# FF1's input operands made one product ahead, and GpSimd without sums, low parts and affine steps up to the early chunks

## The chip, the core and the metric

The kernel runs on one core of a Trainium2 chip. The metric is device time in microseconds for one execution. TensorE (PE) multiplies; VectorE (DVE), ScalarE (ACT) and GpSimd (POOL) do the elementwise work; SyncE (SP) issues the transfers.

## What is computed

One layer of a streaming encoder, 1024 frames by 1024 channels, float32, with conditioning from a vector c. After a first part (projection, retention and gated linear attention, giving `mixed`), what matters here is:

```python
m = mixed @ w_out
x = _layer_norm(ALPHA * x + gate1 * m, ln1_w, ln1_b)
u2 = _layer_norm(x) * (1.0 + scale2) + shift2
f = square(relu(u2 @ w_ff1)) @ w_ff2          # w_ff1 1024 x 4096, w_ff2 4096 x 1024
x = _layer_norm(ALPHA * x + gate2 * f, ln2_w, ln2_b)
```

## The kernel before

**Three products for one.** A float32 product is made as three matmuls of a shorter type. `split` (lines 203 to 206) makes of each operand a high part (a cast on ScalarE, L205) and a low part (source less high part, L206, on VectorE or GpSimd), and `mm3` adds high by high (L211), low by high (L212) and high by low (L213). Inputs have the parts `uhp` and `ulp`, FF1's weights `w1h` and `w1l`.

**Out-projection and norms.** A loop over 8 tiles of 128 frames makes two halves of each by matmuls (`out_part`; VectorE adds x to the half in PSUM and gives y, L838), then takes the first norm of the tile before (`first_norm`, with statistics by bn_stats L200 and L201, a reciprocal root in small steps L181 to L190) and the parameter-free norm (`normed`) of the tile before that. `affine` (L848 to L860) applies the norm's weight and bias to a half, xn: half 0 by ScalarE and two GpSimd steps (L855, L856), half 1 by two VectorE steps (L858, L859). The second norm's statistics (bs<-xn, L200) need both halves.

**The transposed input.** `u2_half(h)` transposes four normed tiles on TensorE (L878) and evicts 8 blocks `ub`, even ones on VectorE (L884), odd ones on ScalarE (L882). Half 0 comes after the out-projection's last tile, half 1 ahead of chunk 2's first products.

**FF1.** w_ff1 is worked through in NC = 8 chunks by a scheme of seven products in place of eight, in the order (1, 2, 5, 6, 7, 3, 4). Products 1 and 2 take blocks of input and weights as they are; the others take sums or differences of blocks, of the input (`RIGHT`) and of the weights (`LEFT`), some of them made in place of an earlier one (`term`, L914). `input_operand(i)` makes the four input operands of product i for all chunks: four sums where it has one (ut, or ub in place), then each one's high and low part. `ff1` makes the two weight operands of a product (w1t or raw in place, then w1h and w1l), and issues its 24 matmuls. After a product VectorE or ScalarE takes the result out of PSUM (`kept`, L1005 and the additions L1019, L1036, L1041), and `hidden` applies relu and square.

**The early chunks.** EARLY = 3: products 1 and 2 of chunks 0, 1 and 2 come first (`ff1_first`), as they need half 0 of the input; then all input operands of products 5, 6, 7, 3 and 4 are made; then follow, chunk by chunk, the five other products (`ff1_rest`, a generator that yields after each product).

**Who does a sum or a low part.** `pick(share)` keeps a running sum of shares and gives a piece to GpSimd whenever the sum reaches 1, otherwise to VectorE. S_U and L_U are the shares for the sums and low parts of the inputs, S_A and L_A for those of the weights of chunks 0 to 2, S_R and L_R for FF2. All pieces count on one running sum.

**Order on an engine.** The program's order gives each piece its place; a scheduler then settles the order of instructions on each engine, and each engine works in order.

Of the kernel before, what the change touches and what calls it, by code (L numbers as in the profile page):

```python
# [13 lines left out]
AF = mybir.ActivationFunctionType  # L14
ALU = mybir.AluOpType
# [13 lines left out]
NRAW = 15  # L29
NLATE = 6  # L30

S_U, L_U = 0.3, 0.3
S_A, L_A = 0.3, 0.3
S_B, L_B = 0.0, 0.2
S_R, L_R = 0.4, 0.4

# [43 lines left out]
def layer_kernel(ctx: ExitStack, tc, x, c, w_ada, b_ada, w_in, ret_norm_w, gla_gate_w, gla_gate_b,  # L80
                 gla_norm_w, w_out, ln1_w, ln1_b, w_ff1, w_ff2, ln2_w, ln2_b, cosT, sinT, cst, out, gam):
    nc = tc.nc
    V, A, G, T = nc.vector, nc.scalar, nc.gpsimd, nc.tensor
# [11 lines left out]
    def nm(s):  # L95
        uid[0] += 1
        return f"{s}_{uid[0]}"
# [10 lines left out]
    def S(shape=(P, HALF), dt=F32, n="s"):  # L108
        tag, bufs = TAGS.get(n, ("S", None))
        return sp.tile(list(shape), dt, tag=tag, name=nm(n), bufs=bufs)  # L110
# [13 lines left out]
    def small(n, tag, bufs=4):  # L124
        return sm.tile([P, n], F32, tag=tag, name=nm(tag))
# [147 lines left out]
    def ada_row(cols, dst):  # L273
        acc = ada_sum(ada_load(cols, ada_late), range(NK))
        yield
        ps = mxt()
        T.matmul(ps, lhsT=ones, rhs=acc, start=True, stop=True)
        br = ada_late()
        nc.sync.dma_start(out=br, in_=b_ada[0:1, cols:cols + HALF].partition_broadcast(P))
        V.tensor_tensor(out=dst, in0=ps, in1=br, op=ALU.add)  # L280
        yield
# [3 lines left out]
    def ada(step):  # L285

        for p in pending:
            next(p)
        pending[:] = [step] if step else []
        for p in pending:  # L290
            next(p)
# [75 lines left out]
    for kind in ("gqk0", "gqk1", "rqk0", "rqk1", "rqk2", "rqk3"):  # L367
        i = int(kind[3])
# [39 lines left out]
    for _ in range(SHARES[0][0]):  # L408
        i = next(steps)
# [334 lines left out]
    row = {}  # L744

    def rowt(name):
        row[name] = [S(n=name), S(n=name)]
        return row[name]
# [92 lines left out]
    def norm_stats(parts):  # L841
        mv, rs = small(2, "mv"), small(1, "rs1")
        stats(parts, mv)
        for _ in row_rsqrt(rs, mv[:, 1:2]):
            pass
        return mv[:, 0:1], rs

    def affine(src, mean, rs, w, b, q):  # L848

        r = S(n="xn")  # L850
        if q == 0:
            nb = small(1, "nb1")
            V.tensor_scalar(out=nb, in0=mean, scalar1=-1.0, scalar2=rs, op0=ALU.mult, op1=ALU.mult)
            A.activation(r, src, AF.Identity, bias=nb, scale=rs)
            G.tensor_tensor(out=r, in0=r, in1=w, op=ALU.mult)  # L855
            G.tensor_tensor(out=r, in0=r, in1=b, op=ALU.add)  # L856
        else:
            V.scalar_tensor_tensor(out=r, in0=src, scalar=mean, in1=w, op0=ALU.subtract, op1=ALU.mult)  # L858
            V.scalar_tensor_tensor(out=r, in0=r, scalar=rs, in1=b, op0=ALU.mult, op1=ALU.add)  # L859
        return r  # L860

    def first_norm(t, ys):

        mean, rs = norm_stats(ys)
        xn = [affine(ys[q], mean, rs, row["ln1_w"][q], row["ln1_b"][q], q) for q in range(2)]
        for q in range(2):
            x1d[t][q] = dr.tile([P, HALF], F32, tag=f"x1d{t}_{q}", name=nm("x1d"))
            nc.sync.dma_start(out=x1d[t][q], in_=xn[q])
        return xn
# [22 lines left out]
    ORDER = (1, 2, 5, 6, 7, 3, 4)  # L892
# [14 lines left out]
    def term(rules, i, blocks, new, share):  # L907

        rule = rules[i]
        if len(rule) == 2:  # L910
            return blocks[rule]
        op, a, b, place = rule
        res = new() if place is None else blocks[place]
        pick(share).tensor_tensor(out=res, in0=blocks[a], in1=blocks[b], op=op)  # L914
        blocks[i] = res
        return res

    def operand(src, new, share):
        hi, lo = new("h"), new("l")
        split(src, hi, lo, lo_eng=pick(share))  # L920
        return hi, lo
# [13 lines left out]
    def load_ff1(c, hh):  # L935
        for kh in range(2):
            for n in range(2):
                w = raw(W1S)
                last_load[0] = nc.sync.dma_start(out=w, in_=w1v[2 * kh + n, :, :, 2048 * hh + 256 * c:2048 * hh + 256 * (c + 1)])
                raw1.setdefault((c, n), {})[hh, kh] = w  # L940

    def input_operand(i):
        bop[i] = []
        for kk in range(4):
            for kh in range(2):
                for th in range(2):
                    usum.setdefault(kk, {})[kh, th] = ub[4 * kh + kk][th]
            src = term(RIGHT, i, usum[kk], lambda: S(n="ut"), S_U)
            bop[i].append(operand(src, lambda s: S(dt=F32R, n="u" + s + "p"), L_U))

    def ff1(c, i, ps, first, last):

        w = []
        for n in range(2):
            src = term(LEFT, i, raw1[c, n], lambda: S(W1S, n="w1t"), S_A if c < EARLY else 0)
            w.append(operand(src, lambda s: S(W1S, F32R, n="w1" + s), L_A if c < EARLY else 0))
        for f in range(2):
            for kk in range(4):
                o = slice(f * P, (f + 1) * P)
                hi, lo = w[kk // 2][0][:, kk % 2, o], w[kk // 2][1][:, kk % 2, o]  # L960
                mm3(ps[f], hi, lo, *bop[i][kk], first and kk == 0, last and kk == 3, True)
# [14 lines left out]
    def hidden(c, hh, th, f, v, src=None):  # L976

        A.activation(v, v if src is None else src, AF.Relu)
        A.activation(v, v, AF.Square)
        g = 2 * c + f  # L980
        b = blocks.setdefault(g, {})
        b[th, hh] = v
        if (th, hh) == (0, 0):
            keep_hidden(g, 1, v)
            if c < EARLY:
                del b[0, 0]
        elif (th, hh) == (1, 1):
            keep_hidden(g, 4, v)
        elif (th, hh) == (1, 0):
            if (0, 0) not in b:  # L990
                b[0, 0] = S(n="c")
                nc.sync.dma_start(out=b[0, 0], in_=hid[g, 1][0])
            for i in (5, 6, 7):
                keep_hidden(g, i, term(LEFT2, i, b, lambda: S(n="c"), 0))
        else:
            keep_hidden(g, 2, v)
            keep_hidden(g, 3, term(LEFT2, 3, b, lambda: S(n="c"), 0))

    def kept(ps, m=None):

        res = S(n="m")
        if m is None:
            A.copy(out=res, in_=ps)
        else:
            V.tensor_tensor(out=res, in0=m, in1=ps, op=ALU.add)  # L1005
        return res

    def two(get):
        return [get() for _ in range(2)]

    def ff1_first(c, keep):

        a, b = two(pjt), two(mxt)
        ff1(c, 1, a, True, keep)
        m = [kept(a[f]) for f in range(2)]
        ff1(c, 2, b, True, True)
        for f in range(2):
            v = S(n="c")
            V.tensor_tensor(out=v, in0=m[f], in1=b[f], op=ALU.add)  # L1019
            hidden(c, 0, 0, f, v)  # L1020
        early[c] = (None, m) if keep else (a, [None, None])

    def ff1_rest(c):

        a, m = early.pop(c)
        fresh = a is None
        a, b = a or two(pjt), two(mxt)
        ff1(c, 5, b, True, False)
        m5 = [kept(b[f], m[f]) for f in range(2)]
        yield  # L1030
        ff1(c, 6, a, fresh, False)
        u2 = [kept(a[f], m[f]) for f in range(2)]
        yield
        ff1(c, 7, a, False, False)
        for f in range(2):
            V.tensor_tensor(out=m5[f], in0=m5[f], in1=a[f], op=ALU.add)  # L1036
            hidden(c, 1, 1, f, m5[f])
        yield
        ff1(c, 3, b, False, True)
        for f in range(2):  # L1040
            V.tensor_tensor(out=u2[f], in0=u2[f], in1=b[f], op=ALU.add)  # L1041
            hidden(c, 0, 1, f, u2[f])
        yield
        ff1(c, 4, a, False, True)
        for f in range(2):
            if m[f] is None:
                hidden(c, 1, 0, f, S(n="c"), a[f])
            else:
                hidden(c, 1, 0, f, kept(a[f], m[f]))
        yield  # L1050
# [111 lines left out]
    ys, x1, xs = {}, {}, {}  # L1162
# [25 lines left out]
        ff1_first(c, True)  # L1188
    for h in range(2):
        load_ff1(0, h)  # L1190
    for i in ORDER[2:]:
        input_operand(i)
    for c in range(NC - 2):
        if c >= EARLY:
            ff1_first(c, False)
        for h in range(2):
            load_ff1(c + 1, h)
        for _ in ff1_rest(c):
            pass
        if c == EARLY:  # L1200
            g2 = rowt("g2")
            with tc.issue_after(last_load[0].ins):
                for q in range(2):
                    ada(ada_row(5120 + HALF * q, g2[q]))
                ada(None)
# [31 lines left out]
    for t in range(NT):  # L1237
        tile_steps = final(t)
        for step in range(4):
            i = next(tile_steps)  # L1240
# [34 lines left out]
```

## Time and profile before

| | us |
|---|---|
| Median of 3 runs (lowest to highest) | 1293.92 (1293.24 to 1295.24) |
| Profiled run | 1295.4 |
| Its span | 1293.6 |
| Mean granted clock of TensorE | 0.973 |

The profile is of one execution; the times of single instructions, waits and stages come from it. "Busy" counts an engine's time in instructions; "idle before" is the time that an engine stood still ahead of an instruction, with what it waited for behind an arrow. A tile's name stands without its number in the trace (uhp), and with it in the lists of instruction order (uhp_6292).

### The profile page before, as it was taken

The numbers are of one execution on the slowest core, as the hardware profiler recorded it, in microseconds if no ns is written. First come the engines' busy times: TensorE is split into PE (matmuls) and PEld (weight loads), VectorE is DVE, ScalarE is ACT, GpSimd is POOL, SyncE is SP. The second block draws the span as 40 slices with busy tenths as digits, with TensorE's granted clock in tenths as the row PEclk, the third lists the DMA queues.
The fourth block names the chain that finished last, engine by engine and source line by source line (L and its number), as shares of the span: only waits on it lengthen the run. The fifth ranks groups of instructions, "written<-read, shape, count | busy, mean of one in ns | idle before, by whom it ended". The sixth has DMA issues, their size and how long they took to land.

```text
span 1293.6 us, 18246 instructions
## 1 busy us (share of the span) xinstructions
PE 1194.6 (92%) x6491; PEld 999.5 (77%) x6491; DVE 968.0 (75%) x1737; ACT 502.2 (39%) x887; POOL 376.5 (29%) x302
## 2 busy tenths in 40 slices
PE   4899899879899989999888999999999899999995
PEld 1587789658887989988676788888888688888784
DVE  6884876798567584377889779877566787897896
ACT  4415322222021332232455446676556445341132
POOL 1333443464143422033344200000002123243236
PEclk9999989989899999999998999999999899999998
DMA  9675210000020122145123668775455455458632
GB/s 316 205 266 186 82 58 21 23 24 25 9 57 25 50 74 82 58 139 187 59 73 115 197 216 303 256 273 188 152 199 177 130 179 189 150 173 292 230 130 98
DMA packets 124124, 183.31 MB, mean 142 GB/s; under 512 B 12337, under 2 KB 52482, under 8 KB 124034
## 3 DMA queue, kind: packets, MB, share of 16 engines
q1 hardware_dynamic: 124034, 182.16, 42.2%
q8 instruction: 51, 0.84, 0.3%
q14 instruction: 39, 0.32, 0.1%
HBM read 137.02 MB, written 45.09 MB: 141 GB/s over the span
## 4 chain that ended last, share of the span: by engine, by line
PE 62%; DVE 9%; issue 2%; POOL 2%; ACT 2%; DMA 1%; DVEq 0%; SPq 0%; POOLq 0%; ACTq 0%
PE pj L211 14%; PE pj L213 14%; PE pj L212 14%; PE mx L212 6%; PE mx L213 6%; PE mx L211 6%; DVE ulp L206 1%; DMA st<-in_w_out 1%; DVE t L648 1%; PE mx L719 1%; PE mx L695 1%; DVE t L647 0%; PE mx L663 0%; DVE t L649 0%; POOL ol L206 0%
## 5 line engine op out<-in xcount | busy, mean ns | idle before, releaser
L211 PE MATMUL pj<-wh,uh 128*128 128x256 f32 (+1 forms) x512 | 146.6, 287 | 0.3 <-ACT wh L205 0.3
L212 PE MATMUL pj<-wl,uh 128*128 128x256 f32 (+1 forms) x512 | 146.0, 285 | 0.7 <-POOL wl L206 0.7
L213 PE MATMUL pj<-wh,ul 128*128 128x256 f32 (+1 forms) x512 | 146.2, 286 | 0.0
L206 POOL TENSOR_TENSOR wl<-st,wh 128x512 fp32r<-128x512 f32 (+1 forms) x60 | 78.5, 1324 | 191.6 <-ACT wh L205 117.0
L211 PE MATMUL pj<-uhp,w1h 128*128 128x512 f32 x256 | 101.7, 399 | 5.3 <-DVE m L1005 3.8
L213 PE MATMUL pj<-uhp,w1l 128*128 128x512 f32 x256 | 100.7, 393 | 0.7 <-POOL w1l L206 0.7
L212 PE MATMUL pj<-ulp,w1h 128*128 128x512 f32 x256 | 100.7, 393 | 0.4 <-POOL ulp L206 0.3
L211 PE MATMUL pj<-bh,ah 128*128 128x512 f32 x256 | 99.8, 391 | 0.8 <-DVE qv L181 0.8
L213 PE MATMUL pj<-bh,al 128*128 128x512 f32 x256 | 99.8, 390 | 0.0
L212 PE MATMUL pj<-bl,ah 128*128 128x512 f32 x256 | 99.8, 390 | 0.0
L212 PEld LDWEIGHTS pj<-wl,uh 128*128 128x128 f32 x512 | 98.2, 192 | 1.3 <-POOL wl L206 0.9
L211 PEld LDWEIGHTS pj<-wh,uh 128*128 128x128 f32 x512 | 98.0, 192 | 1.3 <-ACT wh L205 0.7
L213 PEld LDWEIGHTS pj<-wh,ul 128*128 128x128 f32 x512 | 98.2, 192 | 0.4 <-issue 0.2
L206 POOL TENSOR_TENSOR al<-rh,ah 128x512 fp32r<-128x512 f32 x17 | 26.1, 1534 | 238.9 <-ACT ah L205 214.0
L213 PE MATMUL mx<-uhp,w1l 128*128 128x512 f32 x192 | 76.5, 398 | 6.9 <-DVE w1l L206 6.9
L212 PE MATMUL mx<-bl,ah 128*128 128x512 f32 x192 | 76.0, 396 | 4.1 <-DVE bl L206 4.1
L212 PE MATMUL mx<-ulp,w1h 128*128 128x512 f32 x192 | 76.5, 398 | 2.5 <-POOL ulp L206 1.9
L211 PE MATMUL mx<-bh,ah 128*128 128x512 f32 x192 | 75.8, 396 | 1.3 <-DVE yacc L1106 1.1
L211 PE MATMUL mx<-uhp,w1h 128*128 128x512 f32 x192 | 75.8, 396 | 0.0
L213 PE MATMUL mx<-bh,al 128*128 128x512 f32 x192 | 75.7, 394 | 0.0
L212 PE MATMUL pj<-ul,wh 128*128 128x512 f32 x176 | 71.0, 405 | 4.6 <-DVE ul L206 2.9
L211 PE MATMUL pj<-uh,wh 128*128 128x512 f32 x176 | 71.7, 409 | 2.7 <-ACT uh L205 2.7
(282 smaller groups left out, 3100.1 us busy)
## 6 DMA issues: line engine op xcount, KB each, us to landing
raw<-in_w_ff SPq DMA_DIRECT2D x140, 256.0 KB, 4.0
ada<-in_w_ada SPq DMA_DIRECT2D x96, 256.0 KB, 5.4
rh<-hid SPq DMA_DIRECT2D x84, 256.0 KB, 4.0
hid<-c SPq DMA_DIRECT2D x54, 256.0 KB, 2.4
st<-in_w_in SPq DMA_DIRECT2D x52, 256.0 KB, 3.0
hid<-m SPq DMA_DIRECT2D x30, 256.0 KB, 2.2
hid<-kl SPq DMA_DIRECT2D x28, 256.0 KB, 3.0
hid<-kh SPq DMA_DIRECT2D x28, 256.0 KB, 3.2
```

The source lines that it names most:

```text
L206: (lo_eng or G).tensor_tensor(out=lo, in0=src, in1=hi.bitcast(F32), op=ALU.subtract)
L211: T.matmul(ps, lhsT=lh, rhs=rh, start=first, stop=False, skip_group_check=partial)
L212: T.matmul(ps, lhsT=lh, rhs=rl, start=False, stop=False, skip_group_check=partial)
L213: T.matmul(ps, lhsT=ll, rhs=rh, start=False, stop=last, skip_group_check=partial)
L648: V.tensor_tensor(out=t2[0:64], in0=p[64:128], in1=cs[2 + h][64:128], op=ALU.mult)
L695: T.matmul(op[:, j, :], lhsT=s[:, j, :], rhs=ve(j), start=before[j] is None, stop=True)
L719: T.transpose(out=tp_[:, j * P:(j + 1) * P], in_=ms[j // 2][:, j % 2, i, :], identity=ident)
```

## The change

Three edits. The shares S_U, L_U, S_A and L_A go from 0.3 to 0, so that all of these sums and low parts are VectorE's. `affine` works both halves by the two VectorE steps. And where the input operands of products 5, 6, 7, 3 and 4 were all made ahead of chunk 0's rest, now product 5's are made ahead of it, and within it those of product 6 ahead of product 5, of 7 ahead of 6, of 3 ahead of 7 and of 4 ahead of 3 (`ff1_steps` yields once before the first product, and the loop makes ORDER[n + 3] at its step n).

```diff
--- before.py
+++ after.py
@@ -29,8 +29,8 @@
 NRAW = 15
 NLATE = 6
 
-S_U, L_U = 0.3, 0.3
-S_A, L_A = 0.3, 0.3
+S_U, L_U = 0.0, 0.0
+S_A, L_A = 0.0, 0.0
 S_B, L_B = 0.0, 0.2
 S_R, L_R = 0.4, 0.4
 
@@ -845,24 +845,17 @@
             pass
         return mv[:, 0:1], rs
 
-    def affine(src, mean, rs, w, b, q):
+    def affine(src, mean, rs, w, b):
 
         r = S(n="xn")
-        if q == 0:
-            nb = small(1, "nb1")
-            V.tensor_scalar(out=nb, in0=mean, scalar1=-1.0, scalar2=rs, op0=ALU.mult, op1=ALU.mult)
-            A.activation(r, src, AF.Identity, bias=nb, scale=rs)
-            G.tensor_tensor(out=r, in0=r, in1=w, op=ALU.mult)
-            G.tensor_tensor(out=r, in0=r, in1=b, op=ALU.add)
-        else:
-            V.scalar_tensor_tensor(out=r, in0=src, scalar=mean, in1=w, op0=ALU.subtract, op1=ALU.mult)
-            V.scalar_tensor_tensor(out=r, in0=r, scalar=rs, in1=b, op0=ALU.mult, op1=ALU.add)
+        V.scalar_tensor_tensor(out=r, in0=src, scalar=mean, in1=w, op0=ALU.subtract, op1=ALU.mult)
+        V.scalar_tensor_tensor(out=r, in0=r, scalar=rs, in1=b, op0=ALU.mult, op1=ALU.add)
         return r
 
     def first_norm(t, ys):
 
         mean, rs = norm_stats(ys)
-        xn = [affine(ys[q], mean, rs, row["ln1_w"][q], row["ln1_b"][q], q) for q in range(2)]
+        xn = [affine(ys[q], mean, rs, row["ln1_w"][q], row["ln1_b"][q]) for q in range(2)]
         for q in range(2):
             x1d[t][q] = dr.tile([P, HALF], F32, tag=f"x1d{t}_{q}", name=nm("x1d"))
             nc.sync.dma_start(out=x1d[t][q], in_=xn[q])
@@ -1019,6 +1012,11 @@
             V.tensor_tensor(out=v, in0=m[f], in1=b[f], op=ALU.add)
             hidden(c, 0, 0, f, v)
         early[c] = (None, m) if keep else (a, [None, None])
+
+    def ff1_steps(c):
+
+        yield
+        yield from ff1_rest(c)
 
     def ff1_rest(c):
 
@@ -1188,15 +1186,20 @@
         ff1_first(c, True)
     for h in range(2):
         load_ff1(0, h)
-    for i in ORDER[2:]:
-        input_operand(i)
+    input_operand(5)
     for c in range(NC - 2):
         if c >= EARLY:
             ff1_first(c, False)
         for h in range(2):
             load_ff1(c + 1, h)
-        for _ in ff1_rest(c):
-            pass
+        if c == 0:
+
+            for n, _ in enumerate(ff1_steps(c)):
+                if n < 4:
+                    input_operand(ORDER[n + 3])
+        else:
+            for _ in ff1_rest(c):
+                pass
         if c == EARLY:
             g2 = rowt("g2")
             with tc.issue_after(last_load[0].ins):
```

In the instruction lists VectorE has 1737 rows in place of 1696 (16 affine steps, 33 sums and low parts more, 8 small steps less), GpSimd 257 in place of 306, ScalarE 881 in place of 889, TensorE 5843 in both. Three places show what moved. In them pj and mx are results in PSUM, raw is a block of weights as loaded, st a stage of x.

VectorE before, in the first half's low parts, up to that of block k = 7 of ub (ub_6290):

```order
L206 TENSOR_TENSOR ulp_6379<-ub_6269,uhp_6378 128x512
L853 TENSOR_SCALAR nb_1356_6345<-mv_6329,rs_1350_6330 128x1
L206 TENSOR_TENSOR w1l_6519<-raw_6010,w1h_6518 128x512
L858 SCALAR_TENSOR_TENSOR xn_6350<-y_6185,mv_6329,ln_w_5477 128x512
L206 TENSOR_TENSOR ulp_6383<-ub_6276,uhp_6382 128x512
L859 SCALAR_TENSOR_TENSOR xn_6350<-xn_6350,rs_1350_6330,ln_b_5481 128x512
L200 BN_STATS bs_1363_6360<-xn_6344 128x6
L200 BN_STATS bs_1363_6360<-xn_6350 128x6
L206 TENSOR_TENSOR ulp_6391<-ub_6290,uhp_6390 128x512
```

GpSimd before, at the same place; ub_6262 and ub_6283 are blocks k = 3 and k = 6:

```order
L206 TENSOR_TENSOR ulp_6305<-ub_6262,uhp_6304 128x512
L855 TENSOR_TENSOR xn_6344<-xn_6344,ln_w_5476 128x512
L856 TENSOR_TENSOR xn_6344<-xn_6344,ln_b_5480 128x512
L206 TENSOR_TENSOR ulp_6387<-ub_6283,uhp_6386 128x512
L206 TENSOR_TENSOR w1l_6623<-raw_6014,w1h_6622 128x512
```

VectorE after, at the same place; blocks k = 4, 5 and 6 are ub_6248, ub_6255 and ub_6262:

```order
L188 TENSOR_SCALAR qt_1347_6316<-qt_1347_6316,qv_1345_6314 128x1
L206 TENSOR_TENSOR ulp_6355<-ub_6248,uhp_6354 128x512
L190 TENSOR_SCALAR rs_1343_6309<-qt_1347_6316,qy_1346_6315 128x1
L206 TENSOR_TENSOR ulp_6359<-ub_6255,uhp_6358 128x512
L852 SCALAR_TENSOR_TENSOR xn_6323<-xn_6323,rs_1343_6309,ln_b_5480 128x512
L852 SCALAR_TENSOR_TENSOR xn_6326<-xn_6326,rs_1343_6309,ln_b_5481 128x512
L200 BN_STATS bs_1355_6336<-xn_6323 128x6
L200 BN_STATS bs_1355_6336<-xn_6326 128x6
L206 TENSOR_TENSOR ulp_6363<-ub_6262,uhp_6362 128x512
```

The low part of block 6 moved from GpSimd to VectorE, and stands there behind two closing affine steps (L852) and two bn_stats of the last tile.

VectorE before, where product 5's weights w1l_6847 are made (ulp_6744 to ulp_6759 are inputs of product 6, ulp_6764 of product 7):

```order
L914 TENSOR_TENSOR ut_6730<-ub_6609,ut_6730 128x512
L206 TENSOR_TENSOR ulp_6744<-ut_6718,uhp_6743 128x512
L914 TENSOR_TENSOR ut_6736<-ub_6616,ut_6736 128x512
L206 TENSOR_TENSOR ulp_6749<-ut_6724,uhp_6748 128x512
L914 TENSOR_TENSOR ub_6269<-ub_6269,ut_6718 128x512
L914 TENSOR_TENSOR ub_6283<-ub_6283,ut_6730 128x512
L1019 TENSOR_TENSOR c_6690<-m_6654,mx_6620 128x512
L206 TENSOR_TENSOR ulp_6759<-ut_6736,uhp_6758 128x512
L914 TENSOR_TENSOR ub_6290<-ub_6290,ut_6736 128x512
L206 TENSOR_TENSOR ulp_6764<-ub_6567,uhp_6763 128x512
L206 TENSOR_TENSOR w1l_6847<-w1t_6844,w1h_6846 128x512
```

VectorE after, where product 5's weights w1l_6767 are made (ulp_6715 is an input of product 5, ulp_6736 to ulp_6751 of product 6):

```order
L907 TENSOR_TENSOR ut_6700<-ub_6578,ut_6700 128x512
L206 TENSOR_TENSOR ulp_6715<-ut_6712,uhp_6714 128x512
L907 TENSOR_TENSOR ut_6706<-ub_6585,ut_6706 128x512
L206 TENSOR_TENSOR ulp_6736<-ut_6694,uhp_6735 128x512
L907 TENSOR_TENSOR ut_6712<-ub_6592,ut_6712 128x512
L206 TENSOR_TENSOR ulp_6741<-ut_6700,uhp_6740 128x512
L1012 TENSOR_TENSOR c_6666<-m_6630,mx_6596 128x512
L206 TENSOR_TENSOR ulp_6746<-ut_6706,uhp_6745 128x512
L206 TENSOR_TENSOR w1l_6767<-w1t_6764,w1h_6766 128x512
```

Product 7's sums and inputs stood ahead of product 5's weights, and now stand behind them.

VectorE before, around the additions that take product 7 out of PSUM (m_6874, m_6876, L1036); w1l_6962 and w1l_6967 are weights of product 3:

```order
L206 TENSOR_TENSOR ulp_6805<-ub_6276,uhp_6804 128x512
L206 TENSOR_TENSOR w1l_6962<-raw_6706,w1h_6961 128x512
L1005 TENSOR_TENSOR m_6914<-m_6432,pj_6835 128x512
L206 TENSOR_TENSOR ulp_6815<-ub_6290,uhp_6814 128x512
L206 TENSOR_TENSOR w1l_6967<-raw_6708,w1h_6966 128x512
L914 TENSOR_TENSOR raw_6828<-raw_6820,raw_6828 128x512
L206 TENSOR_TENSOR w1l_7027<-raw_6714,w1h_7026 128x512
L1036 TENSOR_TENSOR m_6874<-m_6874,pj_6834 128x512
L206 TENSOR_TENSOR w1l_7101<-w1t_7098,w1h_7100 128x512
L914 TENSOR_TENSOR w1t_7098<-w1t_7098,raw_6818 128x512
L1036 TENSOR_TENSOR m_6876<-m_6876,pj_6835 128x512
```

VectorE after, around the same additions (m_6794, m_6796, L1034); raw_6682 and w1l_6938 are weights of product 3:

```order
L1034 TENSOR_TENSOR m_6794<-m_6794,pj_6754 128x512
L206 TENSOR_TENSOR ulp_6923<-ub_6255,uhp_6922 128x512
L907 TENSOR_TENSOR ub_6269<-ub_6269,ut_6712 128x512
L206 TENSOR_TENSOR ulp_6928<-ub_6262,uhp_6927 128x512
L1034 TENSOR_TENSOR m_6796<-m_6796,pj_6755 128x512
L206 TENSOR_TENSOR ulp_6933<-ub_6269,uhp_6932 128x512
L907 TENSOR_TENSOR raw_6682<-raw_6682,w1t_6758 128x512
L907 TENSOR_TENSOR raw_6684<-raw_6684,w1t_6764 128x512
L907 TENSOR_TENSOR w1t_7080<-raw_6728,raw_6732 128x512
L206 TENSOR_TENSOR w1l_6938<-raw_6682,w1h_6937 128x512
```

Product 3's weights stood ahead of product 7's additions; now their sums and low parts stand behind them.

## Rows read from the trace of the kernel before

**Rows 1.** The page: busy time of each engine, share of the span, instructions.

```profile
PE 1194.6 (92%) x6491; PEld 999.5 (77%) x6491; DVE 968.0 (75%) x1737; ACT 502.2 (39%) x887; POOL 376.5 (29%) x302
```

**Rows 2.** Windows: range, length, busy us (count) PE, PEld, DVE, ACT, POOL; clock, DMA, GB/s.

```profile
603.00:625.00 22.00, 22.00 (x98) 18.04 (x98) 15.62 (x44) 5.82 (x10) 7.20 (x6) 1.00 0.15 58
625.00:660.00 35.00, 30.04 (x136) 22.83 (x135) 25.73 (x52) 21.25 (x38) 7.80 (x7) 0.95 0.25 83
644.00:649.00 5.00, 5.00 (x17) 3.90 (x16) 2.23 (x9) 2.60 (x5) 1.28 (x1) 0.66 0.33 105
660.00:726.00 66.00, 54.69 (x245) 44.01 (x243) 61.08 (x76) 35.42 (x62) 31.22 (x21) 0.95 0.38 123
726.00:760.00 34.00, 33.92 (x141) 27.57 (x142) 24.79 (x36) 13.70 (x25) 5.17 (x4) 0.95 0.60 203
```

**Rows 3.** Waits of PE, 540 to 760 us: total us, times, longest.

```profile
PE mx L213 <- DVE w1l L206: 6.9, 1, 6.9
PE pj L211 <- DVE m L1005: 3.8, 2, 2.7
...
PE pj L211 <- ACT uhp L205: 0.7, 1, 0.7
PE pj L213 <- POOL w1l L206: 0.7, 1, 0.7
```

**Rows 4.** Timeline of DVE at the out-projection's end: start us, us, ..., [idle before].

```profile
617.91 0.69 DVE L838 SCALAR_TENSOR_TENSOR y<-st,pj 128x512 f32<-128x512 f32 x1 [0.22 <-PE pj L213]
...
621.02 0.74 DVE L858 SCALAR_TENSOR_TENSOR xn<-y,mv,ln_w 128x512 f32<-128x512 f32 x1
621.80 0.75 DVE L859 SCALAR_TENSOR_TENSOR xn<-xn,rs,ln_b 128x512 f32<-128x512 f32 x1
...
625.11 0.69 DVE L200 BATCH_NORM_STATS2 bs<-xn 128x6 f32<-128x512 f32 x1 [1.83 <-POOL xn L856]
...
628.28 0.68 DVE L838 SCALAR_TENSOR_TENSOR y<-st,pj 128x512 f32<-128x512 f32 x1
628.87 1.52 DVE L884 TENSOR_SCALAR ub<-mx,keep 128x512 f32<-128x512 f32 x2
```

**Rows 5.** Timeline of PE, first transposes and product 2 of chunk 0.

```profile
625.22 3.22 PE L878 MATMUL mx<-keep,x1n 128*128 128x128 f32 x28
...
643.36 0.50 PE L212 MATMUL mx<-ulp,w1h 128*128 128x512 f32 x1 [1.85 <-POOL ulp L206]
```

**Rows 6.** Timeline of PE, product 5 of chunk 0 to product 7 of chunk 1.

```profile
673.86 0.39 PE L211 MATMUL mx<-uhp,w1h 128*128 128x512 f32 x1
...
675.45 0.39 PE L212 MATMUL mx<-ulp,w1h 128*128 128x512 f32 x1
682.77 0.80 PE L213 MATMUL mx<-uhp,w1l 128*128 128x512 f32 x1 [6.93 <-DVE w1l L206]
683.36 0.63 PE L211 MATMUL mx<-uhp,w1h 128*128 128x512 f32 x1
...
722.96 0.39 PE L213 MATMUL pj<-uhp,w1l 128*128 128x512 f32 x1
726.08 0.47 PE L211 MATMUL pj<-uhp,w1h 128*128 128x512 f32 x1 [2.73 <-DVE m L1005]
...
727.39 0.63 PE L212 MATMUL pj<-ulp,w1h 128*128 128x512 f32 x1
```

**Rows 7.** Timeline of DVE, second half of the transposed input.

```profile
660.25 1.53 DVE L884 TENSOR_SCALAR ub<-mx,keep 128x512 f32<-128x512 f32 x2
...
672.64 1.78 DVE L914 TENSOR_TENSOR ub<-ub,ub 128x512 f32<-128x512 f32 x1
674.34 0.68 DVE L206 TENSOR_TENSOR ulp<-ut,uhp 128x512 fp32r<-128x512 f32 x1
674.94 0.68 DVE L914 TENSOR_TENSOR ut<-ub,ut 128x512 f32<-128x512 f32 x1
```

**Rows 8.** The page: TensorE's low-part matmuls of FF2, busy, mean ns | idle.

```profile
L212 PE MATMUL mx<-bl,ah 128*128 128x512 f32 x192 | 76.0, 396 | 4.1 <-DVE bl L206 4.1
```

## The prediction

> **What bounds the kernel now.** The page comes first: TensorE is busy for 92% of the span and VectorE for 75% [rows 1]. Such shares are means over stages, so the second look is at busy time by stage. At the end of the out-projection TensorE is never idle; from 625 to 660 us it works 30.04 of 35 us; from 660 to 726 it works 54.69 of 66 us while VectorE works 61.08; from 726 on it is busy again and VectorE has a quarter of its time free [rows 2]. So whatever this change is worth, it is worth it between 625 and 726 us, where VectorE and GpSimd prepare the operands of FF1's early chunks. The third look is at what ends TensorE's waits there: a low part of weights (w1l, L206) for 6.9 us once, two kept sums (m, L1005) for 3.8, and a low part on GpSimd for 0.7 [rows 3]; the first stretch adds a wait of 1.85 for a low part of GpSimd's [rows 5].
>
> The fourth look is at the rows themselves, since a wait has a tail. A matmul of 512 columns starts some 0.23 us after the last one (673.86 is the first of product 5, 675.45 the eighth). From 675.45 to 682.77 are 7.32 us, so 7.1 are lost, and then each matmul lasts 0.63 us and not 0.39 [rows 6] and starts 0.2 later than it would, for some 3 us: TensorE runs at the lower of its two clock levels, 1.2 GHz. Seven or eight such steps cost another 1.5 us. The wait that ends at 726.08 loses 2.9 (3.12 from start to start) and is followed by the same, about 1.6 [rows 6]; the one that ends at 643.36 loses 2.0, and the five us after 644 hold 17 matmuls in place of 22, at a mean granted clock of 0.66 and until 648, some 1.6 in all [rows 2, 5]. The shorter waits of [rows 3], 0.7 and 3.8 - 2.7 = 1.1 long, have no such tail.
>
> **Part 1: the norm's affine step.** In the out-projection VectorE runs behind TensorE. From one y to the corresponding y a tile later it takes 628.28 - 617.91 = 10.4 us, and in this stands one wait of 1.83 us for GpSimd's xn [rows 4]. The change puts two more scalar_tensor_tensor there, 0.78 us from one start to the next [rows 4], and takes away the wait and a small step of 0.2. As a sum: 10.4 - 1.83 - 0.2 + 1.56 = 9.9, or a little less, because one of the new steps stands where the reciprocal waits for ScalarE. TensorE needs 48 x 0.23 = 11.0 us for a tile, and is fully busy then [rows 2], so VectorE gains 1 us or more on it with every tile. It was some 2.9 us late at the last one (TensorE is on to the transposes at 625.22, y starts at 628.28) [rows 4, 5], and should now be level: y at 625.8, the first ub at 626.4 in place of 628.87. That the added 1.3 us a tile cost TensorE nothing rests on this cover of 11.0 against 9.9; were it gone, the eight tiles could cost up to eight times the excess.
>
> **Part 2: the low parts of the first half.** Product 2 of chunk 0 waited until 643.36 for an ulp of GpSimd's, which stood there behind its two affine steps [rows 5]. In the new order all eight stand on VectorE, but the one in question comes behind the last tile's two closing affine steps and two bn_stats, as the order of the change shows. From the first ub: four ub at 0.72, seven low parts ahead of it (one of them of weights) at 0.60, four affine steps at 0.77, three bn_stats at 0.60 and six small steps at 0.2 to 0.25 make 13.4 us: it begins at 639.8 and ends at 640.4. That is 3.0 us before 643.36. TensorE still meets a wait of 2 us or so there; the nearest row is the wait of 2.0 that lost the clock [rows 5], so I keep the 1.6 us of its tail. **Gain 3.0** (bounds: 1.5, if ScalarE's casts hold VectorE up twice by the 0.7 that TensorE waits for one [rows 3]; 5, if the tail goes too).
>
> **Part 3: the middle.** VectorE's instructions cost two prices. Beside GpSimd they start 1.70 us apart (672.64 to 674.34); when GpSimd is silent, 0.60 apart (674.34 to 674.94) [rows 7]. Between 660 and 726 VectorE did 76 instructions in 61.08 us and GpSimd 21 in 31.22 [rows 2]. The new order has 95 in their place, all on VectorE: at 0.60 they take 57 us in place of 66. The Trainium skill has a rule for this ("SBUF — State Buffer", Who interferes with whom): a VectorE instruction with two SBUF inputs and a GpSimd instruction that reads SBUF share a port, and the second to come is blocked wholly. By that rule the slow rows end with GpSimd's work, and the trace agrees with 1.78 us against 0.68 for the same subtraction; it shows no stretch of 95 at 0.60.
>
> What it does to each wait. From the first ub of the second half (660.25 before, 657.25 now) 18 instructions stand ahead of product 5's last low part of the inputs: four of 0.76 and fourteen of 0.60, 11.4 us. Product 5 starts 13.6 us after that ub, at 673.86 [rows 6], so its operands are there and the 7.1 us go. The reason is the new order: before, operands of products 6, 7 and 3 stood ahead of w1l_6847.
>
> What is late next: each later product's sums of weights now stand behind additions that wait for TensorE. Product 6: w1t is in line behind a kept m, and its high and low parts follow; 0.6 + 0.6 for the two, a cast of 0.5, less what is already under way: 1.7. Product 7, behind one addition: 0.6. Product 3: raw_6682 is in line behind m_6796, which waits for product 7's last matmul; then 0.1 + 0.6 + 0.6 + 0.7 and a cast of ScalarE (0.7 is what TensorE waits for one [rows 3]) come before its first matmul: 2.7 to 2.8. Chunk 1's product 7: 0.15. Together 5.1, and I take it that the 2.8 loses the clock like 2.0 and 2.9 did: 1.5. Against that, before: 7.1 + 1.5 + 0.8 + 1.3 + 2.9 + 1.6 = 15.2. **Gain 15.2 - 6.6 = 8.6.** Bounds for the new waits: 2 us (if the scheduled places suit, no tail) and 10 us (each 1.5 times that with a second tail). A test from the other side: TensorE's own work from product 5 to chunk 1's product 7 is 726.08 - 673.86 less 13.6 lost = 38.6; 670.9 + 38.6 + 6.6 = 716.1, and VectorE's 95 instructions end at 657.25 + 57 = 714.3 at the earliest. The two are within 2 us: VectorE is nearly a bound still.
>
> **Part 4: the rest.** From 726 on VectorE had 24.79 busy of 34 us [rows 2]; the low parts of chunks 1 and 2 that it takes over (36 instructions at 0.6 = 21.6 us for a chunk whose 120 matmuls take 27) lie beside TensorE. Loads keep their order on SP. FF2's dealing is a running sum that now starts from another remainder, so its low parts change engine by one place. FF2's second set has two waits of 4.1 us in all for such parts [rows 8], with the pipeline's filling and one tail some 6: that pair could vanish or a like one appear. Taken at 0, bounds -6 and +6.
>
> **Sum.** 3.0 + 8.6 = 11.6. Profiled run 1295.4 (span 1293.6) to 1283.8; the median of the three runs is 1.5 lower, so 1293.92 - 11.6 = 1282.3.
>
> **Rivals.** (a) VectorE becomes the bound. Each instruction lasts 0.68 although the next starts after 0.60; if mixed dependences and waits for ScalarE make the mean step 0.68, 95 take 64.6 us, chunk 1's product 7 starts at about 722 in place of 726, and the gain is 4 to 6: 1289. For it: VectorE is within 2 us of the bound by the test above. Against: runs of 0.60 in the trace, dependent or not, as long as GpSimd is silent. The Trainium skill has advice that would reverse the change ("Perfetto Trace Analysis", Optimizing Scalar/DVE Operations): from a saturated VectorE, work may be offloaded even to GpSimd; it adds that the shared port may make it useless. (b) Slower: the step is 0.78, as between the dependent pair of affine steps [rows 4]. Then 95 take 74 us, product 7 of chunk 1 starts at 731 and not 726, and the time is 1297 to 1299. It decides from a mean step of 0.725 = (726.08 - 657.25) / 95. Against: only those pairs stand so far apart, and few of the 95 are pairs of that kind. (c) FF2's remainder adds a pair of waits: 1288; takes one away: 1276. (d) The norm's work isn't hidden: with the wait for GpSimd gone but the reload of c from memory or ScalarE's casts late, only the 7.1 us stall goes and others take its place: within 2.5 of before.
>
> **How the numbers follow.** Forecast with its bounds, 1278 to 1286: 0.6. (a) 0.16. (c) up 0.06, down 0.05. (d) 0.07. (b) 0.06. Some 0.2% (2.6 us) is about what a measurement of this kernel tells from no change. Faster by more: 0.6 + 0.16 + 0.06 + 0.05 = 0.87; within: 0.07; slower: 0.06. The range leaves out (b), (d) and the lower part of (c): 1277 to 1290.
>
> **What would show it.** In the new trace: no GpSimd work between the first norm and FF1's end; VectorE rows 0.60 apart from 657 to 714 (a mean over 0.65 speaks for (a)); the first ub near 626.4; no 7 us wait in product 5, and the longest in the middle ahead of product 3; chunk 1's product 7 near 716. A first ub after 628 would make part 1 wrong, a wait over 3 us at products 6 or 7 part 3, and a gap in FF2 where there was none part 4.

## Result and profile after

| | before | after |
|---|---|---|
| Median, us (runs) | 1293.77 (4: 1293.24 to 1295.24) | 1276.87 (4: 1275.61 to 1277.63) |
| Ratio, 95% interval | | 0.9868 [0.9847, 0.9890] |
| Profiled run, span | 1295.4, 1293.6 | 1275.61, 1273.8 |

The change makes the kernel 16.9 us faster; a later measurement on another occasion gave 0.9883 [0.9861, 0.9905], some 15 us by that ratio and 13 by the medians (1279.83 against 1292.81). The forecast was 1282.3, with a range of 1277 to 1290. The mechanisms were those forecast, except that the first of the two stretches gained far more.

Of the 19.8 us between the profiled spans, 1.4 lie before the out-projection, where nothing was changed (TensorE is on to the transposes at 623.83 and not 625.22), so the two stretches are counted from there. The windows of after answer [rows 2], with the same columns:

```profile
603.00:625.00 22.00, 22.00 (x103) 18.21 (x102) 17.74 (x47) 3.63 (x9) 0.00 (x0) 1.00 0.13 48
625.00:660.00 35.00, 34.84 (x179) 28.86 (x178) 29.52 (x58) 26.96 (x49) 0.00 (x0) 1.00 0.27 91
660.00:726.00 66.00, 61.77 (x265) 48.82 (x265) 63.62 (x106) 36.98 (x65) 0.00 (x0) 1.00 0.52 170
726.00:760.00 34.00, 34.00 (x150) 27.80 (x149) 27.31 (x45) 17.07 (x30) 0.00 (x0) 1.00 0.61 199
```

From 625 to 660 TensorE works 34.84 of 35 us where it worked 30.04; GpSimd is silent; the granted clock is 1.00 in all four. VectorE has 106 instructions in the 66 us where it had 76. TensorE's waits from 540 to 760 us, beside [rows 3], are down to three:

```profile
PE mx L211 <- ACT w1h L205: 2.7, 1, 2.7
PE pj L211 <- ACT w1h L205: 1.1, 1, 1.1
PE pj L211 <- DVE m L998: 0.4, 1, 0.4
```

VectorE's timeline at the out-projection's end and after it, beside [rows 4]:

```profile
613.04 0.69 DVE L838 SCALAR_TENSOR_TENSOR y<-st,pj 128x512 f32<-128x512 f32 x1 [1.70 <-PE pj L213]
...
624.03 0.69 DVE L838 SCALAR_TENSOR_TENSOR y<-st,pj 128x512 f32<-128x512 f32 x1 [1.76 <-PE pj L213]
624.63 1.52 DVE L877 TENSOR_SCALAR ub<-mx,keep 128x512 f32<-128x512 f32 x2
...
634.40 1.41 DVE L852 SCALAR_TENSOR_TENSOR xn<-xn,rs,ln_b 128x512 f32<-128x512 f32 x2
635.72 1.29 DVE L200 BATCH_NORM_STATS2 bs<-xn 128x6 f32<-128x512 f32 x2
636.92 0.68 DVE L206 TENSOR_TENSOR ulp<-ub,uhp 128x512 fp32r<-128x512 f32 x1
```

Now VectorE waits for TensorE with its y, 1.7 us a tile, and the last y starts 0.2 us behind the start of the transposes and not 3.1. The low part of block 6 starts at 636.92, 13.1 us behind that start; the forecast had it at 639.8 - 625.2 = 14.6. TensorE's timeline in the middle, beside [rows 6]:

```profile
671.43 0.50 PE L211 MATMUL pj<-uhp,w1h 128*128 128x512 f32 x1 [1.13 <-ACT w1h L205]
...
683.45 0.40 PE L213 MATMUL pj<-uhp,w1l 128*128 128x512 f32 x1
686.54 0.51 PE L211 MATMUL mx<-uhp,w1h 128*128 128x512 f32 x1 [2.69 <-ACT w1h L205]
686.88 0.39 PE L212 MATMUL mx<-ulp,w1h 128*128 128x512 f32 x1
```

The 7 us wait of product 5 is gone; 2.9 us are lost ahead of product 3 (from start to start, 683.45 to 686.54, less the 0.23 of a matmul; "lost" is counted so throughout), and the matmuls behind that last 0.39 us: the clock did not fall.

### The profile page after: what moved, and what is told of

Same layout as the page of the kernel before. It is cut to its first block, busy times and chain, and to the rows that moved or that the text cites. A ratio compares the mean times of both kernels' runs of the same rounds, so it can differ in the third digit from the quotient of the medians.

```text
span 1273.8 us, 18210 instructions
## 1 busy us (share of the span) xinstructions
PE 1187.6 (93%) x6491; PEld 993.7 (78%) x6491; DVE 965.2 (76%) x1778; ACT 496.4 (39%) x879; POOL 301.0 (24%) x253
```

## Experiments

**The edits one by one and in pairs.** Six kernels: each edit of the change alone, and the change without each. The diffs are those of the change; for the order alone, for instance:

```diff
-    for i in ORDER[2:]:
-        input_operand(i)
+    input_operand(5)
...
+            for n, _ in enumerate(ff1_steps(c)):
+                if n < 4:
+                    input_operand(ORDER[n + 3])
```

e_affine, e_shares, e_order (alone); x_order (affine and shares), x_affine (shares and order), x_shares (affine and order):

> The kernel before with the affine edit alone. Theory A (each edit has a place of its own; the affine edit frees GpSimd and VectorE at the end of the out-projection and lets TensorE's order run on in the first stretch): the first ub is 1.5 to 2.5 us earlier, the waits of the stretch up to 650 us shrink by 5 to 8 us, the waits of product 5 (7 us) and of chunk 1's product 7 (3 us) stay; 1286 to 1289. Rival B (the slow pairs of VectorE and GpSimd alone are the cause): GpSimd still has its sums and low parts, so little changes: 1292 to 1294.

> The kernel before with the four shares at 0 alone. Theory A: y stays late by the wait for xn, so the first stretch gains only 2 to 4; VectorE's rows in the middle go to 0.60 us, but product 5's second low part of weights is still 36 rows behind the first ub of the second half, 22 us at 0.60 where TensorE wants it after 15.2, so a wait of about 7 us stays in product 5, and those behind it shrink: 1283 to 1287. Rival B: contention was the cause, the wait in product 5 falls under 2 us: 1278 to 1281.

> The kernel before with the input operands one product ahead alone, shares at 0.3. Theory A: the wait of product 5 goes (7 us), but VectorE and GpSimd have the same 76 and 21 instructions at the same slow pace up to chunk 1's product 7, so that starts at 722 to 727 us and the wait comes back at products 6, 7 and 3: 1290 to 1294. Rival C (the place of product 5's weights was the cause, the pace of VectorE doesn't matter): 1284 to 1286.

> The changed kernel with all input operands made ahead of chunk 0's rest again. Theory A: the first stretch keeps its gain of 8 us, product 5 waits 7 to 8 us again and loses the clock for 1.5, and the waits of products 6, 7 and 3 (4.7 us in the changed kernel) go: 1279 to 1282. Rival B: 1276 to 1278, since nothing but contention mattered. Rival C: 1284 or more, the order being worth the 8 us or more that it removes at product 5 with no return.

> The changed kernel with the old affine step (half 0 by ScalarE and GpSimd). Theory A: y of the last tile is late again by about 2.5 us and so are the first ub and low parts; the first stretch loses 4 to 6 of its 8 us, the middle keeps its gain: 1281 to 1283. Rival B (what counts is contention in the middle, the affine step is hidden): 1277 to 1278.

> The changed kernel with the four shares at 0.3 again. Theory A: the first stretch keeps 5 to 7 us of its gain, the middle gains 0 to 2 over the kernel before, since the slow pairs set its pace: 1285 to 1288. Rival C (the order alone made the middle's gain): 1277 to 1280.

Beside the times the table has two lengths taken from the traces, by counting matmuls: A, from the first transposes to product 5 of chunk 0; B, from there to product 7 of chunk 1.

| edits | median, us | ratio to before [95%] | A | B |
|---|---|---|---|---|
| none (two profiles) | 1293.2 | 1 | 48.6, 46.3 | 52.2, 52.1 |
| affine | 1291.12 | 0.9982 [0.9969, 0.9995] | 41.6 | 52.9 |
| shares | 1287.36 | 0.9948 [0.9930, 0.9965] | 44.0 | 47.8 |
| order | 1296.81 | 1.0030 [1.0019, 1.0042] | 47.4 | 54.7 |
| affine, shares | 1282.10 | 0.9918 [0.9890, 0.9946] | 40.8 | 47.7 |
| shares, order | 1283.70 | 0.9933 [0.9908, 0.9958] | 44.0 | 44.1 |
| affine, order | 1291.75 | 0.9984 [0.9969, 0.9999] | 41.7 | 55.5 |
| all | 1276.87 | 0.9868 [0.9847, 0.9890] | 40.8 | 44.2 |

A is settled by the affine edit (alone 7.0 us against the first profile of before, 4.7 against the second), with a part of the shares' (alone 4.6 and 2.3). B is settled by the shares, and by the order only with them: alone, the order makes B 2.5 us longer, with the shares 3.6 shorter. So theory A of the expectations stands best: its times hold within 1 us for the three kernels with the shares at 0, and were 2 to 4 us too low for the three without. For the affine edit alone the time is even nearer to rival B (1292 to 1294); there it is stretch A that speaks for theory A. That contention alone mattered (B) falls with product 5's wait in e_shares and x_order, and the order alone (C) with e_order. The order alone shows why. TensorE's timeline of e_order at products 6 and 7:

```profile
682.18 0.80 PE L211 MATMUL pj<-uhp,w1h 128*128 128x512 f32 x1 [5.07 <-ACT w1h L205]
682.78 0.63 PE L212 MATMUL pj<-ulp,w1h 128*128 128x512 f32 x1
...
695.11 0.72 PE L211 MATMUL pj<-uhp,w1h 128*128 128x512 f32 x1 [4.12 <-DVE m L1005]
695.63 0.63 PE L212 MATMUL pj<-ulp,w1h 128*128 128x512 f32 x1
```

Product 5's wait went, and came back as 5.1 at product 6 and 4.1 at product 7, both with matmuls of 0.63 us behind them: VectorE was as slow as before, 72 instructions in 61.04 us beside 21 of GpSimd's (before: 76 in 61.08). The window of e_order, with the columns of [rows 2]:

```profile
660.00:726.00 66.00, 55.27 (x223) 43.78 (x221) 61.04 (x72) 33.38 (x59) 31.19 (x21) 0.92 0.37 118
```

And with the shares but the old order (x_order) product 5 waits again:

```profile
674.08 0.79 PE L213 MATMUL mx<-uhp,w1l 128*128 128x512 f32 x1 [5.67 <-DVE w1l L206]
674.67 0.63 PE L211 MATMUL mx<-uhp,w1h 128*128 128x512 f32 x1
```

**How stable the stretches are.** The kernel before and the affine edit alone were profiled again.

> The kernel before, a second profile. If the waits and tails that the sum set against each other stand fast, the stretch from the first transposes to product 5 is again 48 to 49 us and that to chunk 1's product 7 52 to 53, with a tail of 1.3 to 1.7 us at the lower clock behind three waits. If the tails come and go, both are up to 3 us shorter, and the gain of the change was counted too high by that.

> The kernel before with the affine edit alone, a second profile. If its first stretch of 41.6 us stands fast (7 us under the kernel before) its time of only 2 us under that one needs another 4 to 5 us somewhere behind chunk 1's product 7, which was 1.6 us over the kernel before's in the first profile; otherwise the first stretch is 44 us or more.

Before: 1292.84, A 46.3 and B 52.1 (its transposes start 4.9 us later, at 630.16, in a profiled run that took 1298.6). The affine edit: 1289.55, A 41.7 and B 52.6, at a ratio of 0.9980 [0.9962, 0.9997]. The edit's stretches stand fast. Before's A doesn't. TensorE's timeline of the second profile has the wait of [rows 5] again, but behind it matmuls of 0.40 and 0.39 us; the slow ones, of 0.63 us, come earlier here, in product 1 (granted clock 0.66 from 636 to 641 us):

```profile
637.88 0.63 PE L213 MATMUL pj<-uhp,w1l 128*128 128x512 f32 x1
638.30 0.63 PE L211 MATMUL pj<-uhp,w1h 128*128 128x512 f32 x1
...
647.58 0.50 PE L212 MATMUL mx<-ulp,w1h 128*128 128x512 f32 x1 [1.86 <-POOL ulp L206]
647.91 0.40 PE L213 MATMUL mx<-uhp,w1l 128*128 128x512 f32 x1
```

So a stretch at the lower clock stands in both profiles of before, at another place: it cost 1.6 us in the first and 1.3 in the second. Of the 2.4 us between the two A's the other 2 are short waits, at 628.2, 636.3 and 639.5 us of the first profile, that are shorter or missing in the second. The gain in A is 5.5 to 7.9 us.

From chunk 1's product 7 to the end of the span the affine kernel takes 2.0 to 2.4 us more than before's first profile and 1.2 to 1.6 more than its second, though it has no tail of 1.7 there; so its time shows less than its stretches. Against the first profile 1.9 to 2.4 us go between 1180 and 1235 us, where TensorE waits for a cast of FF2's weights (bh), 2.4 us in one profile of the affine kernel and 1.4 in the other, 0.3 and 1.3 in those of before, and 1.2 us behind TensorE's last matmul. The edit changes nothing there, and why these grew was not tested.

**TensorE's order.** pe_fixed holds products 1 and 2 of chunks 0 and 1 to the program's order on TensorE:

```diff
         for f in range(2):
-            for kk in range(4):
+            with tc.issue_after(last_mm[0].ins) if c < 2 and i < 3 and last_mm else nullcontext():
+                for kk in range(4):
...
+            last_mm[:] = [mm]
```

> The changed kernel, with TensorE's products 1 and 2 of chunks 0 and 1 held to the program's order (first half of the columns, then the second, chunk 0 then chunk 1), where the changed kernel lets matmuls whose operands are there go ahead of one that waits for the low part of block 6. Theory D (that the first stretch gained 8 us and not 3 comes from TensorE's new order): TensorE waits 2 to 3 us in product 2 of chunk 0, with or without a tail of 1.6 us at the lower clock: 1279 to 1282, most of the 5 us that the forecast missed. Rival E (the low parts came early enough by themselves): within 1 us of the changed kernel, 1276 to 1278.

1280.16, ratio 0.9903 [0.9887, 0.9920]: 3.3 us over the changed kernel's first measurement and level with its second (1279.83), so the time by itself settles nothing. The traces do: A is 43.8 where the two profiles of the changed kernel have 40.8 and 40.7, and B 44.1. Theory D has the size right and the place wrong. TensorE's timeline of pe_fixed:

```profile
630.15 0.51 PE L212 MATMUL pj<-ulp,w1h 128*128 128x512 f32 x1 [1.13 <-DVE ulp L206]
...
631.75 0.79 PE L212 MATMUL pj<-ulp,w1h 128*128 128x512 f32 x1 [0.48 <-DVE ulp L206]
632.35 0.63 PE L213 MATMUL pj<-uhp,w1l 128*128 128x512 f32 x1
```

It waits for the first two low parts of product 1, 1.4 and 0.7 us lost, and then matmuls of 0.63 us, at 1.2 GHz, up to 634.9 cost another 1.5 (granted clock 0.87 from 625 to 634 us); block 6's low part is there in time. In the changed kernel four matmuls of high parts go first (627.24 to 628.8), two of them chunk 1's, and only 0.7 us is lost there.

But the kernel before has these four first as well, ahead of its first low part:

```profile
630.38 0.73 PE L211 MATMUL pj<-uhp,w1h 128*128 128x512 f32 x2 [0.71 <-ACT uhp L205]
...
633.08 0.50 PE L212 MATMUL pj<-ulp,w1h 128*128 128x512 f32 x1
```

So this run shows what an order can be worth, and not what is new in the changed kernel's. That can be counted in the traces and the instruction lists. The first matmul with block 6's low part is the 34th behind the first transposes in the kernel before (643.36, [rows 5]) and the 44th in the changed kernel (638.03):

```profile
637.35 0.39 PE L211 MATMUL mx<-uhp,w1h 128*128 128x512 f32 x1
637.58 0.39 PE L213 MATMUL pj<-uhp,w1l 128*128 128x512 f32 x1
637.80 0.39 PE L211 MATMUL pj<-uhp,w1h 128*128 128x512 f32 x1
638.03 0.39 PE L212 MATMUL mx<-ulp,w1h 128*128 128x512 f32 x1
```

Of the ten that now pass it, seven are of product 2's other half of columns and three of chunk 1's. They take 2.3 us, and the low part is done at 636.92 + 0.68 = 637.60.

**GpSimd's reading and writing.** g_read adds 24 GpSimd additions to the changed kernel beside the operands of products 5, 6 and 7, whose results nobody uses; g_write puts a memset in their place, behind an addition of one column; g_read2 and g_write2 do the same into one tile of their own.

```diff
+            if i in (5, 6, 7):
+                for e in range(2):
+                    gx = S(n="gx")
+                    G.tensor_tensor(out=gx, in0=usum[kk][1, 1], in1=usum[kk][1, 1], op=ALU.add)
```

> The changed kernel with 24 GpSimd additions of two inputs in SBUF, 128x512, whose results nobody reads, four pairs each beside the input operands of products 5, 6 and 7; the orders of VectorE and TensorE are those of the changed kernel. Theory A (the slow rows are paid for GpSimd's reading at the same time): VectorE's rows beside them are 1.3 to 1.8 us apart, it loses 0.7 to 1.1 us for each of the 24, and since it has nothing to spare before chunk 1's product 7 the time grows by 15 to 22 us: 1292 to 1299. Rival (the slow pace of before came from the order and the waits, not from GpSimd): within 2 us of the changed kernel.

> The same with 24 GpSimd memsets of 128x512, which write and read nothing, each behind an addition of one column. Theory A: VectorE keeps its 0.60 us beside the memsets and the time stays within 2 us of the changed kernel: 1275 to 1279. Rival (any work on GpSimd slows VectorE): 1285 or more.

> The same with 24 GpSimd additions of two inputs of 128x512 in SBUF. Theory A: VectorE's rows with two inputs in SBUF go to 1.45 us beside them, as in the run with buffers, and the stretch from product 5 to chunk 1's product 7 grows from 44 by 15 to 20 us: 1293 to 1299. Rival (it was the wait for buffers): under 1286.

> The changed kernel with 24 GpSimd memsets of 128x512, each behind an addition of one column, all into one tile of their own, so that no cast of ScalarE waits for a buffer; the orders of VectorE, ScalarE and TensorE are those of the changed kernel. Theory A (what slows VectorE is GpSimd's reading): 1276 to 1281, the stretch from product 5 to chunk 1's product 7 within 1 us of 44.2. Rival (any GpSimd work slows VectorE): that stretch over 50 us.

g_read took 1298.14 us, ratio 1.0039 [1.0023, 1.0054], as theory A had it; B grew from 44.2 to 63.8. GpSimd's and VectorE's timelines of it:

```profile
653.92 34.30 POOL L946 TENSOR_TENSOR gx<-ub 128x512 f32<-128x512 f32 x24 [144.75 <-DVE ub L877]
```

```profile
669.89 1.52 DVE L907 TENSOR_TENSOR ut<-ub,ut 128x512 f32<-128x512 f32 x1
671.34 1.52 DVE L206 TENSOR_TENSOR ulp<-ut,uhp 128x512 fp32r<-128x512 f32 x1
672.79 0.67 DVE L1016 TENSOR_TENSOR c<-m,mx 128x512 f32<-128x512 f32 x1
673.38 0.93 DVE L206 TENSOR_TENSOR ulp<-ut,uhp 128x512 fp32r<-128x512 f32 x1
```

Steps with two inputs in SBUF start 1.45 us apart in place of 0.60; the one with an input in PSUM (c<-m,mx) lasts 0.67 among them. Nineteen steps that lose 0.85 and five that lose 0.25 to 0.4 make 17.6 of the 19.6 us by which B grew.

The times of the other three miss theory A: 1286.47 (0.9932) for g_write, 1297.35 (1.0034) for g_write2, 1300.34 (1.0048) for g_read2. By time alone the rival, that any GpSimd work slows VectorE, would stand. But in these runs the extra work made others wait for it. In g_write ScalarE's cast waited 5.3 us for a memset's buffer, in g_write2 VectorE stood 16.3 us behind the last memset, and in g_read2 5.4. What they show is the pace, which in g_read2 is 1.45 again. ScalarE's cast, GpSimd's memsets and VectorE's rows beside these in g_write:

```profile
667.79 0.62 ACT L205 CAST uhp<-ut 128x512 fp32r<-128x512 f32 x1 [5.33 <-POOL gx L947]
```

```profile
667.23 10.34 POOL L947 MEMSET gx<- 128x512 f32 x22
```

```profile
669.12 0.68 DVE L206 TENSOR_TENSOR w1l<-w1t,w1h 128x512 fp32r<-128x512 f32 x1
669.72 0.68 DVE L206 TENSOR_TENSOR ulp<-ut,uhp 128x512 fp32r<-128x512 f32 x1
670.33 0.68 DVE L1017 TENSOR_TENSOR c<-m,mx 128x512 f32<-128x512 f32 x1
```

Beside memsets VectorE keeps its 0.60 us. So GpSimd's reading sets the slow pace, and not GpSimd's work as such.

A GpSimd read can also be the one that stands. In g_write2 an addition of one column, 0.19 us by itself, took 7.57 us beside VectorE's steps with two inputs in SBUF, which kept their 0.60, and ended just behind the start of the next one with an input in PSUM. GpSimd's row, then VectorE's:

```profile
657.14 7.57 POOL L947 TENSOR_TENSOR gx<-ub 128x1 f32<-128x1 f32 x1
```

```profile
663.96 0.69 DVE L206 TENSOR_TENSOR ulp<-ut,uhp 128x512 fp32r<-128x512 f32 x1
664.57 0.68 DVE L1018 TENSOR_TENSOR c<-m,mx 128x512 f32<-128x512 f32 x1
```

That is part of why the memsets came late. Why the two engines take turns in g_read and not here was not tested.

**The waits that are left.** w_ahead1 makes the weight operands of products 6, 7, 3 and 4 of chunk 0 one product ahead too; w_ahead_ub besides takes four evictions from VectorE (the first of these two places):

```diff
-            if k % 2:
+            if k % 2 or h:
...
         ff1(c, 6, a, fresh, False)
+        if c < AHEAD:
+            weights(c, 7)
         u2 = [kept(a[f], m[f]) for f in range(2)]
```

> The changed kernel, with the weight operands of products 6, 7, 3 and 4 of chunk 0 also made one product ahead, ahead of the additions that take the product before out of PSUM. Theory F (the three waits left in the middle, 1.3, 0.6 and 2.9 us, are there because these sums stand behind additions that wait for TensorE): the three shrink to 1 us or less in all, 1272 to 1274. Rival G (VectorE is the bound there, so the wait only moves to another product): 1275.5 to 1277.5.

> The changed kernel with the weights of products 6, 7, 3 and 4 of chunk 0 one product ahead, and with all eight blocks of the second half of the transposed input evicted by ScalarE, four of them VectorE's before (some 2.9 us). Theory G (VectorE is the bound up to chunk 1's product 7; it was busy 54.65 of 55 us there with the weights ahead): what is taken from it comes off the wait at chunk 1's product 7 (2.3 us), so 1 to 3 us under the changed kernel: 1274 to 1276. Rival H (ScalarE's longer queue delays the casts of product 5): no better than the changed kernel, or 1 to 2 us worse.

> The changed kernel once more, beside the next one on the same chip: 1275.5 to 1278. Its trace is a second look at the stretches: from the first transposes to product 5 some 41 us, from there to chunk 1's product 7 some 44 (theory A), and whether a wait of about 2.9 us ahead of product 3 again leaves the clock up; the forecast's step was that it falls.

w_ahead1: 1275.48, ratio 0.9869 [0.9854, 0.9884], the changed kernel's own; B 41.7. The three waits shrank to 0.6 us lost, and a new one of 2.3 came at chunk 1's product 7, with VectorE busy 54.65 of 55 us: F is right on the place and G on the outcome. Its window:

```profile
652.00:707.00 55.00, 52.41 (x240) 42.76 (x239) 54.65 (x91) 35.38 (x62) 0.00 (x0) 1.00 0.40 132
```

w_ahead_ub: 1273.32, ratio 0.9841 [0.9821, 0.9860], beside 1279.83 and 0.9883 [0.9861, 0.9905] for the changed kernel on the same chip (A 40.7 and B 44.2 there, as expected, the time 1.8 us above the 1275.5 to 1278). Theory G stands, with a little more gain than it gave; its B of 38.7 is TensorE's own work, which the prediction had at 38.6. Its windows:

```profile
654.00:705.00 51.00, 51.00 (x235) 42.06 (x233) 50.52 (x85) 35.67 (x63) 0.00 (x0) 1.00 0.41 136
705.00:760.00 55.00, 54.98 (x241) 44.84 (x240) 48.71 (x80) 27.33 (x48) 0.00 (x0) 1.00 0.69 231
```

TensorE has no wait left there, and VectorE is busy 50.52 of 51 us. It beats both kernels in median, the changed one beside it by 6.5 us; their intervals against before do not overlap, if barely. The interval of the changed kernel's first measurement does overlap; against that one it is B that decides, 38.7 against 44.2.

## Why the prediction was right or wrong

**Part 1, the affine step, was right.** The first ub came 0.8 us behind the start of the transposes (forecast 1.2, before 3.6), and the out-projection took TensorE 88.7 us in both profiles, so the added steps cost it nothing. (The last y of before was 3.1 us late, where the prediction reads 2.9.)

**Part 2 failed.** It gave the first stretch 3.0 us; the traces give 7.9, or 5.5 against the second profile of before. The step that failed is "TensorE still meets a wait of 2 us or so there", with its tail of 1.6 kept: it held TensorE's order as it was while VectorE's was worked through row by row. In the old order the wait would indeed have been there: ten matmuls earlier TensorE would have come to block 6's low part at 638.03 - 2.3 = 635.8, 1.8 us before it was done. In the new order those ten, chunk 1's among them, fill the place, and no matmul behind it runs at the lower clock.

Besides, block 6's low part came 1.5 us earlier than summed. The first ub gave 0.4 of it; in the sum from there, 13.4 us and measured 12.3, the four affine steps took 0.66 each and not 0.77, and a small step ahead of a large one takes 0.12 us (632.23 to 632.35) and not 0.2 to 0.25.

Against the first profile of before, the 4.9 us that were missed are then some 1.8 for the wait, 1.6 for the tail and 1.5 for the low part. This division is an estimate from the rows: no run put the old order of TensorE into the changed kernel. pe_fixed, held to the program's order, loses 3.1 us, but at product 1.

**Part 3 was right in mechanism and near in size.** VectorE's pace was 0.60 as taken (93 instructions from 651 to 708 us, in the window below), and the waits left were 1.3, 0.6, 2.9 and 0 against 1.7, 0.6, 2.8 and 0.15. Only the 1.5 us tail behind the 2.8 did not come. The gain was 8.0 in B and 1.6 in the tail that before has behind 726.08, against 8.6 in all. The runs confirm both halves of the argument: the pace (g_read) and the place of product 5's weights (x_order).

```profile
651.00:708.00 57.00, 52.77 (x239) 42.01 (x238) 56.51 (x93) 35.41 (x62) 0.00 (x0) 1.00 0.41 134
```

**Part 4.** The rest was level, to 1 or 2 us in either direction from trace to trace.

**Rivals.** (a) and (b) fall with the pace of 0.60. The nearness that (a) spoke of was real: with the weights ahead as well, VectorE was the bound (w_ahead1). (c) and (d) did not come: FF2's second set still has its waits, now 1.4 and 1.2 us lost, with a shorter one (0.6 and 0.8 in the two profiles) and slow matmuls behind them.

The profiled run lies 8.2 us under the 1283.8 forecast for it: 4.9 are part 2's, 1.0 part 3's, and 2.3 lie before the out-projection (1.4) and behind the middle (0.9), where the prediction set nothing; those are chance as far as is known, since the out-projection starts anywhere from 534.6 to 541.5 us in these traces. The sum was too small by 2.5 to 5 us in part 2, so that 1276.87 lies just under the range, whose lower end had no room for a tail-free first stretch and middle together; the second measurement, 1279.83, lies in it.

## What to carry over

Work through the waiting engine's new order too, not only the one that feeds it: a scheduler that moves low parts also lets ready matmuls pass waiting ones, ten of them here. When two engines share work and one slows the other, give the slow one's share back and shorten the queue ahead of the first consumer in the same change: one of the two alone was worth 6 us here, and the other alone cost 4. Where a kernel's traces differ in a tail at the lower clock, take it as a range and not as a term.

## What the hardware showed

A wait's length did not tell whether the clock fell. One that lost 2.0 us was followed by matmuls of 0.63 us in one profile of the kernel before (643.36) and not in the other, where such matmuls stood ahead of it; and 2.1 us lost in e_shares were followed by matmuls of 0.40:

```profile
641.63 0.50 PE L212 MATMUL mx<-ulp,w1h 128*128 128x512 f32 x1 [1.97 <-DVE ulp L206]
641.96 0.40 PE L213 MATMUL mx<-uhp,w1l 128*128 128x512 f32 x1
```

2.9 us lost cost 1.7 in the kernel before (726.08) and 0.3 in the changed kernel (686.54), in both of its profiles; 1.4 us lost at 630 us in pe_fixed, with 0.7 behind it, cost 1.5. What decides was not settled.

A VectorE step with an input in PSUM keeps its pace beside GpSimd's reads (0.67 us against 1.52 for steps with two inputs in SBUF). The Trainium skill states this too ("SBUF — State Buffer", Who interferes with whom): with at most one SBUF input, and outside the two-port modes, a VectorE instruction doesn't contend with GpSimd, and one with two SBUF inputs doesn't contend with a GpSimd instruction that only writes. g_read's and g_write's rows agree.
